# Value projection of cached samples moved into a feed-forward block, key products on one engine, finals two steps apart

## The chip, the cores and the metric

The kernel runs on one core of a Trainium2 chip. The time is device microseconds of one execution. The core has five engines that each work through their own list of instructions in order: TensorE (PE, matmuls), VectorE (DVE), ScalarE (ACT), GpSimd (POOL) and SyncE (SP), which here issues all the DMAs. The engines meet at semaphores.

## The reference

One layer of a hybrid decoder for 2048 prompt tokens and 32 sample rows (8 samples with 4 new tokens each), D = 1024, everything in float32:

```python
z = rmsnorm(x, g) @ w_in                     # -> q, k, v (8 heads x 64), u, vg (512 each)
# attention in three branches (window, dilation) = (128,1), (512,4), (2048,16),
# merged by their softmax denominators; samples see a cache of 2048 keys and values:
s = einsum('bthc,btjhc->bthj', q, k_all[:, idx]) * 64**-0.5 + bias
o = einsum('bthj,btjhc->bthc', exp(s - lse), v_all[:, idx])
gate = einsum('gts,...sgc->...tgc', tril(w_s), layernorm(vg)) + b_s
x = x + concat(att, u * gate) @ w_out
x = x + (silu(h @ w_gate) * (h @ w_up)) @ w_down     # h = rmsnorm(x, g), 2816 hidden columns
y = rmsnorm(x, final_g)
```

The outputs are y for prompt and samples, the prompt's keys and values, the samples' caches moved on by four rows, and the samples' normalised vg.

## The kernel before

Each float32 product is made of three matmuls: both operands are split into a high part (a copy rounded for PE, on ACT) and a low part (original minus high, on DVE or POOL). The order on every engine is written out by hand: the scheduler only adds the semaphores. The stages are these.

- **Input projection**, 240 steps of one 128-row slice of `w_in` against three or so token tiles, a little over two microseconds each. The rest of the stage's work is put at steps by `at(step, phase, function)`: a `Plan` sorts by step, then by phase ("early", "turn", "mid", "out", "misc", "store" among ten), and calls the functions in that order. The functions only append to the engines' lists. Here also lie the spatial gate (layer norm, split into `vnh`, `vnl`, gate matmuls L426, eviction `gates_u` L434) and the samples' attention.
- **Samples' attention.** 96 key units (8 samples x 4 tokens x 3 branches): a product of cached keys with the broadcast query on DVE or POOL (L555), and a sum over each head's 64 columns on DVE (L560). Two softmaxes follow for four samples each. Then 72 value units (9 for a sample: one near piece, and far and middle pieces for 4 tokens): load of 96 to 128 rows x 512, high part on ACT (L629), low part on DVE or POOL (L635), two matmuls (L644, L645) that add into one PSUM bank for the nine. The stationary operand is the split probabilities (`z0`, `z1`); a mask and a small selecting matmul make the sample's four output rows of it.
- **Prompt attention**, then three token **blocks** of 6, 6 and 4 tiles. Each has output projection, second norm and the feed-forward's gate and up products. These go by 22 slices `f` of the hidden columns, and a slice has seven products `q` = 0..6 (a Strassen form): a *slot* is one product, 12 matmuls of 384 columns in the first block (L1686 to L1688). Each slot's product is evicted or added by DVE or ACT (L1698 q = 1, L1700 q = 2, L1710 q = 3, L1713 and L1714 q = 4, L1716 q = 5, L1723 and L1748 q = 6), and between them lie the operand sums (L1603 to L1612, DVE), high parts (L1619, ACT) and low parts (L1623, POOL) for the next slice.
- **Down projection** of all blocks (class `Down`): stages of ten steps with 12 matmuls each. Step `n` also splits the operands of step `n + 3` (L1883 to L1886); after each stage the first four steps evict its four banks, and in the last stages of each half they also start a final norm each (`final`, L1811, L1457, L1818).

Small PSUM tiles come from `ps_t()`, which takes the banks in `ring` in turn. `roll(1)` copies a piece of up to 512 KB of the samples' cache from input to output, DRAM to DRAM.

Of the kernel before, what the change touches and what calls it, by code (L numbers as in the profile page):

```python
# [66 lines left out]
def hymba_step(ctx: ExitStack, tc: tile.TileContext, A: dict, O: dict):  # L67
# [55 lines left out]
    t_d = dram.tile([NJ, 2, P, 2, 512], F32, name="t_d")  # L123
    x1_d = dram.tile([T, D], F32, name="x1_d")
# [359 lines left out]
    bias_s = gp.tile([P, 3, 1, ST * H], F32, name="bias_s")  # L484
# [40 lines left out]
    sel = sp.tile([2 * SR, ST], F32, name="sel")  # L525
# [36 lines left out]
    def sample_start():  # L562
        dve.memset(S, 0.0)
        sync.dma_start(sel, A["sel"])

    def values_start():


        unit["z0"] = z0 = sp.tile([P, 2, ST, 2, ST, H], F32R, name="z0", tag="kn", bufs=2)
        dve.memset(z0.bitcast(F32), 0.0)  # L570

    def head_mask():
        unit["hm"] = sp.tile([P, DA], F32, name="hm", tag="kn", bufs=2)[0:2 * SR]
        sync.dma_start(unit["hm"], A["headmask"])
# [24 lines left out]
    def softmax_c(bg):  # L599
# [4 lines left out]
        unit["pT", bg] = pT = sp.tile([P, 3, 4, ST, H], F32, name="pT", tag="pT", bufs=1)  # L604
        act.activation(pT.rearrange("p u b t h -> p (u b t h)"), pt[:, 0:3 * P], AF.Copy)

    def probabilities(b):
        pT = unit["pT", b // 4]
        bi = b % 4
        z0 = unit["z0"]  # L610
        for u in range(2):

            hi = bass.AP(tensor=z0.tensor, offset=z0.offset + u * ST * 2 * SR, ap=[list(z0.ap[0]), [2 * SR + H, ST], [1, H]])
            lo = bass.AP(tensor=z0.tensor, offset=z0.offset + u * ST * 2 * SR + SR, ap=[list(z0.ap[0]), [2 * SR + H, ST], [1, H]])
            dve.tensor_copy(hi, pT[:, u, bi])
            dve.tensor_sub(lo, pT[:, u, bi], hi.bitcast(F32))

    def near_probabilities(b):
        pT = unit["pT", b // 4]
        bi = b % 4  # L620
        unit["z1"] = z1 = sp.tile([P, 2, ST * H], F32R, name="z1", tag="z1", bufs=1)
        src = pT[:, 2, bi].rearrange("p t h -> p (t h)")
        dve.tensor_copy(z1[:, 0, :], src)
        dve.tensor_sub(z1[:, 1, :], src, z1[:, 0, :].bitcast(F32))

    def value_unit_split(b, i, u, t):
# [11 lines left out]
    def value_unit(b, i, u, t):  # L638
        vh, vl, n = unit.pop(("vs", b, i))
        if i == 0:  # L640
            unit["po"] = ps_t(1)
# [1184 lines left out]
    class Down:  # L1826
# [98 lines left out]
        def run(self):  # L1925
            for n in range(2 * NS - TAIL):
# [495 lines left out]
```

## Time and profile before

| | before |
|---|---|
| runs: median (lowest to highest) | 2494.89 us (2493.87 to 2495.75) |
| profiled execution, its time | 2493.14 us |
| profiled execution, span from first to last instruction | 2491.4 us |
| mean granted PE clock | 0.992 |

The span by stages, with PE's busy time, from the table by stretches:

| stretch, us | stage | length | PE busy | DVE | ACT | POOL |
|---|---|---|---|---|---|---|
| 0–575 | input projection | 575 | 548.4 | 338.8 | 257.3 | 216.3 |
| 575–935 | prompt attention | 360 | 321.8 | 289.4 | 260.0 | 207.1 |
| 1000–1310 | block 1 of 3, gate and up | 310 | 309.9 | 188.2 | 116.4 | 198.9 |
| 1410–1735 | block 2 of 3, gate and up | 325 | 324.3 | 231.1 | 125.5 | 222.7 |
| 1815–2070 | block 3 of 3, gate and up | 255 | 255.0 | 169.1 | 136.0 | 198.0 |
| 2070–2491 | down projection, finals | 421.4 | 401.3 | 320.1 | 190.3 | 7.6 |

In the rows below, `L635 DVE TENSOR_TENSOR vl<-kv,vh` is an instruction of line 635 on DVE that writes `vl` from `kv` and `vh`. A row of a list of waits ends with three numbers: the time that the engine waited for this in all, how often, and the longest. A row of the timeline begins with its start in us and its length, and ends, in brackets, with the time its engine had been idle and what ended that. A row of a group ends with its count, busy us and mean ns of one, and the idle time ahead of it with what released it.

### The profile page before, as it was taken

Reading aid. Unit: us, or ns where it says so; the run is one execution under the profiler, and the core shown is the slowest. Engines: PE = TensorE matmul, PEld = TensorE weight load, DVE = VectorE, ACT = ScalarE, POOL = GpSimd, SP = SyncE. Lnnn points to the kernel's source line nnn. Section 1 sums busy time; section 2 is a strip of 40 time slices with the busy share of each in tenths; the row PEclk is TensorE's granted clock in tenths of the full one; section 3 lists DMA queues with packets and bytes.
Section 4 is the critical chain, followed back from the end, with each engine's and each line's share of the span. In section 5 each row is a group of like instructions: output and inputs, shape, how many; then the busy total and the mean of one; then the engine's idle time right before and its main releaser. Section 6 shows DMA issues by size and latency. Waiting matters only on the chain. (4 is left out here: it accounts for less than half of the span.)

```text
span 2491.4 us, 39127 instructions
## 1 busy us (share of the span) xinstructions
PE 2397.9 (96%) x13358; PEld 2120.8 (85%) x13358; DVE 1691.0 (68%) x3081; ACT 1211.9 (49%) x2385; POOL 1183.7 (48%) x909
## 2 busy tenths in 40 slices
PE   8999999999989889999999999999999999999997
PEld 6787777778888777999998899999799998887886
DVE  4368686446878777656655776776566666877876
ACT  6414344546877656433333633334455554445444
POOL 1145643224575746666663576666467881000000
PEclk9999999999999999999999999999999999999999
DMA  8863854788788665566659177666647776755832
GB/s 265 255 202 112 275 147 140 246 278 265 232 281 259 218 185 171 190 212 207 202 200 320 36 250 255 231 243 226 255 151 229 234 221 235 279 186 197 318 128 89
DMA packets 315221, 537.17 MB, mean 216 GB/s; under 512 B 28417, under 2 KB 151714, under 8 KB 309134
## 3 DMA queue, kind: packets, MB, share of 16 engines
q1 hardware_dynamic: 310060, 526.16, 64.6%
q10 hardware_dynamic: 4962, 8.51, 1.3%
q8 instruction: 106, 1.74, 0.3%
q14 instruction: 93, 0.76, 0.1%
HBM read 418.41 MB, written 186.28 MB: 243 GB/s over the span
## 5 line engine op out<-in xcount | busy, mean ns | idle before, releaser
L1686 PE MATMUL ps_m<-xh,op 128*128 128x384 f32 (+5 forms) x1932 | 612.3, 317 | 0.8 <-DVE raw L1714 0.5
L1687 PE MATMUL ps_m<-xl,op 128*128 128x384 f32 (+5 forms) x1932 | 612.0, 317 | 0.0
L1688 PE MATMUL ps_m<-xh,op 128*128 128x384 f32 (+5 forms) x1932 | 611.3, 316 | 0.0
L1623 POOL TENSOR_TENSOR op<-fr,op 128x512 fp32r<-128x512 f32 x286 | 402.6, 1424 | 91.7 <-ACT op L1619 65.0
L1686 PEld LDWEIGHTS ps_m<-xh,op 128*128 128x128 f32 x1932 | 363.9, 188 | 2.4 <-issue 0.8
L1687 PEld LDWEIGHTS ps_m<-xl,op 128*128 128x128 f32 x1932 | 363.8, 188 | 0.6
L1688 PEld LDWEIGHTS ps_m<-xh,op 128*128 128x128 f32 x1932 | 364.2, 188 | 0.0
L1623 POOL TENSOR_TENSOR op<-pair,op 128x512 fp32r<-128x512 f32 x126 | 169.6, 1347 | 158.3 <-DVE hr L1748 87.1
L1619 ACT ACTIVATE op<-fr 128x512 fp32r<-128x512 f32 x330 | 196.6, 621 | 12.2 <-PE ps_m L1438 6.0
L335 PE MATMUL ps_s<-wh,xh 128*128 128x512 f32 x480 | 195.8, 408 | 6.1 <-ACT xh L139 6.1
L336 PE MATMUL ps_s<-wl,xh 128*128 128x512 f32 x480 | 189.9, 396 | 0.0
L337 PE MATMUL ps_s<-wh,xl 128*128 128x512 f32 x480 | 189.5, 395 | 0.1
L1737 ACT ACTIVATE ps_t<-zn 128x384 f32<-128x384 f32 (+2 forms) x132 | 60.0, 454 | 250.4 <-DVE zn L1716 205.5
L1883 ACT ACTIVATE op<-fr 128x512 fp32r<-128x512 f32 x140 | 88.3, 631 | 173.9 <-issue 89.2
L1955 POOL TENSOR_TENSOR ac<-ac,final_g 128x512 f32<-128x512 f32 x2 | 2.6, 1296 | 351.9 <-DMA fr<-t_d 349.3
L1885 DVE TENSOR_TENSOR op<-fr,op 128x512 fp32r<-128x512 f32 x140 | 99.3, 710 | 80.4 <-ACT op L1883 80.1
L1619 ACT ACTIVATE op<-pair 128x512 fp32r<-128x512 f32 x126 | 79.0, 627 | 110.9 <-DVE pair L1609 110.9
L335 PEld LDWEIGHTS ps_s<-wh,xh 128*128 128x128 f32 x480 | 91.5, 191 | 34.5 <-issue 7.3
L1900 PE MATMUL ps_m<-op 128*128 128x512 f32 x280 | 109.0, 389 | 0.9 <-ACT op L1884 0.9
L1902 PE MATMUL ps_m<-op 128*128 128x512 f32 x280 | 109.1, 390 | 0.2
L337 PEld LDWEIGHTS ps_s<-wh,xl 128*128 128x128 f32 x480 | 91.5, 191 | 20.8 <-POOL xl L142 0.5
L1901 PE MATMUL ps_m<-op 128*128 128x512 f32 x280 | 109.0, 389 | 0.0
(551 smaller groups left out, 5942.0 us busy)
## 6 DMA issues: line engine op xcount, KB each, us to landing
fr<-in_w_gate_dram SPq DMA_DIRECT2D x132, 256.0 KB
out_ks_dram<-in_cache_k_dram SPq DMA_DIRECT2D x56, 512.0 KB
out_vs_dram<-in_cache_v_dram SPq DMA_DIRECT2D x56, 512.0 KB
fr<-in_w_up_dram SPq DMA_DIRECT2D x110, 256.0 KB
fr<-ab_d SPq DMA_DIRECT2D x88, 256.0 KB
a<-h_d SPq DMA_DIRECT2D x80, 256.0 KB
fr<-t_d SPq DMA_DIRECT2D x80, 256.0 KB
raw<-in_w_in_dram SPq DMA_DIRECT2D x72, 256.0 KB
```

What stands on the lines that cost most here:

```text
L335: pe.matmul(o[j], xh[:, k, :], wh, start=(k == 0), stop=False)
L336: pe.matmul(o[j], xh[:, k, :], wl, start=False, stop=False)
L337: pe.matmul(o[j], xl[:, k, :], wh, start=False, stop=(k == KD - 1))
L1619: act.activation(ops[f, j][0], ab[f][j], AF.Copy)
L1623: (eng or pool).tensor_sub(lo_, ab[f][j], hi.bitcast(F32))
L1686: pe.matmul(out, wh[:, ks], xh[:, :, k], start=(k == 0), stop=False)
L1687: pe.matmul(out, wh[:, ks], xl[:, :, k], start=False, stop=False)
L1688: pe.matmul(out, wl[:, ks], xh[:, :, k], start=False, stop=(k == 3))
L1885: dve.tensor_sub(wl, w, wh.bitcast(F32))
L1900: pe.matmul(banks[m], hh[:, ts], wh, start=first, stop=False, skip_group_check=more)
L1901: pe.matmul(banks[m], hh[:, ts], wl, start=False, stop=False, skip_group_check=more)
L1902: pe.matmul(banks[m], hl[:, ts], wh, start=False, stop=j == NJ - 1, skip_group_check=more)
```

## The change

- **Value units.** Loads, splits and matmuls of the 72 units leave steps 160 to 241 of the input projection. They now stand in the first block's slices 1 to 21: with `x = 7 f - 7 + q`, unit `k` has its two matmuls in slot `9 + 16k // 9`, straight after that slot's product. Its high part (ACT) is two slots earlier, its low part one slot earlier and always on DVE, its load in the slot before that of unit `k - 2`, whose staging buffer it takes. The probabilities go through a DRAM tile `p_d`. The mask is 64 x 8 and is broadcast over each head's columns.
- **Key units.** All 96 products are on DVE (57 were on POOL). From the thirteenth on they stand at steps 63, 64.9, 66.8 … 222, where before they came in bursts of 0.4 to 1.7 a step up to step 162. The softmaxes stand at steps 150 and 227 (158 and 189 before).
- **Banks.** The ring for `ps_t` is [0, 1] up to step 168 and [0, 1, 3] up to 240. Before it was [0] from 165 and [0, 3] from 168, since the values held bank 1.
- **Rolls.** 21 cache copies go from the first block to steps 172 to 222 of the input projection.
- **Samples' gate.** The load and the eight small transposes of the samples' gate values go from the prompt attention to the second block's slice 19.
- **Finals.** `Down` evicts the four banks of a stage at steps 0, 2, 4 and 6 of the next (0 to 3 before), and the finals go with them. The four little tiles of squares share one.

PE's order around the gates of step 166 to 168, before and after (the number behind `ps_t` is the bank; `vnh` is the layer norm's high part, `wg_h` the gate's weights, `vh`, `vl` a value unit). Before:

```order
L426 MATMUL ps_t0_3515<-vnh_3276,wg_l_107 128x256
L335 MATMUL ps_s_3365<-wh_3079,xh_2810 128x512
...
L337 MATMUL ps_s_3365<-wh_3079,xl_2863 128x512
L426 MATMUL ps_t0_3553<-vnh_3276,wg_h_106 128x256
...
L337 MATMUL ps_s_3365<-wh_3096,xl_2863 128x512
L644 MATMUL ps_t1_3570<-vh_3476,z1_3449 64x512
L645 MATMUL ps_t1_3570<-vl_3497,z1_3449 64x512
L335 MATMUL ps_s_3585<-wh_3398,xh_2305 128x512
```

After:

```order
L427 MATMUL ps_t0_3331<-vnh_3118,wg_l_108 128x256
L336 MATMUL ps_s_3201<-wh_2915,xh_2684 128x512
...
L338 MATMUL ps_s_3201<-wh_2915,xl_2737 128x512
L427 MATMUL ps_t1_3359<-vnh_3118,wg_h_107 128x256
...
L338 MATMUL ps_s_3201<-wh_2937,xl_2737 128x512
L336 MATMUL ps_s_3386<-wh_3233,xh_2220 128x512
```

The second gate's bank changes from 0 to 1, and the value unit's two matmuls behind it are gone.

DVE's order a few steps later, past the gates (`om` is a sample's masked output, `z` its probabilities, `un` the gated u). Before:

```order
L635 TENSOR_TENSOR vl<-kv,vh 128x512
L649 TENSOR_TENSOR om<-ps_t_3570,hm 64x512
L615 CAST z_3209<-pT 128x4x8
L616 TENSOR_TENSOR z_3209<-pT,z_3209 128x4x8
...
L635 TENSOR_TENSOR vl<-kv,vh 100x512
L434 SCALAR_TENSOR_TENSOR un<-ps_o_3833,sgb,un 128x4x64 x2
```

After:

```order
L555 TENSOR_TENSOR pr<-kv,qb 96x512
L560 TENSOR_REDUCE S_s<-pr 96x8
L555 TENSOR_TENSOR pr<-kn,qb 128x512
L435 SCALAR_TENSOR_TENSOR un<-ps_o_3586,sgb,un 128x4x64 x2
L560 TENSOR_REDUCE S_s<-pr 128x8
L555 TENSOR_TENSOR pr<-kv,qb 100x512
```

Values' low parts and probabilities make room for key products (L555) and their sums (L560).

DVE's order in the first block at the turn from one slice to the next (`zn`, `raw` and `hr` are the products' evictions and the hidden values, `pair` and `fr` the operand sums of the next slice). Before:

```order
L1716 TENSOR_TENSOR zn<-zn,ps_m_10982 128x384
L1748 TENSOR_TENSOR hr<-ps_t_10996,raw 128x3x2x64
L1723 TENSOR_TENSOR raw<-raw,ps_m_11002 128x384
L1748 TENSOR_TENSOR hr<-ps_t_10934,raw 128x3x2x64
L1603 TENSOR_TENSOR pair<-fr 128x512
L1606 TENSOR_TENSOR fr<-fr 128x512
L1698 TENSOR_TENSOR raw<-zn,ps_m_11048 128x384
```

After (L2213 is a value unit's low part, lines 1645 and 1670 were 1723 and 1748, line 1525 was 1603, line 1620 was 1698):

```order
L1638 TENSOR_TENSOR zn<-zn,ps_m_10440 128x384
L1670 TENSOR_TENSOR hr<-ps_t_10454,raw 128x3x2x64
L1645 TENSOR_TENSOR raw<-raw,ps_m_10463 128x384
L1670 TENSOR_TENSOR hr<-ps_t_10378,raw 128x3x2x64
L2213 TENSOR_TENSOR svb<-sva,svb 100x512
L1525 TENSOR_TENSOR pair<-fr 128x512
L1528 TENSOR_TENSOR fr<-fr 128x512
L1620 TENSOR_TENSOR raw<-zn,ps_m_10514 128x384
```

A low part stands between the slice's last eviction and the first operand sum; its matmuls on PE (L2221, L2222) come after the next product.

The diff, cut to its core:

```diff
-    for s0, r in ((165, [0]), (168, [0, 3]), (B0, [0, 1])):
+    for s0, r in ((168, [0, 1, 3]), (B0, [0, 1])):
...
-    key_steps = [46 + 5 * i // 4 for i in range(8)] + [60, 61, 61, 62] + [63 + int(i / 1.7) for i in range(17)]
-    key_steps += [73 + int(i / 1.2) for i in range(12)] + [83 + int(i / 0.4) for i in range(11)] + [111 + int(i / 0.95) for i in range(32)]
-    key_steps += [145 + int(i / 0.7) for i in range(12)]
+    key_steps = [46 + 5 * i // 4 for i in range(8)] + [60, 61, 61, 62] + [63 + 19 * i // 10 for i in range(84)]
...
-        at(s0, "out", key_unit, b, t, u, pool if u == 1 or u == 2 and not 83 <= s0 < 111 and s0 < 150 else dve)
+        at(s0, "out", key_unit, b, t, u, dve)
...
-    V0 = 166
     for bg in range(2):
-        s0 = (V0 - 8, V0 + 23)[bg]
+        s0 = (150, 227)[bg]
+        at(s0 - 1, "early", sample_bias, bg)
         at(s0, "turn", softmax_a, bg)
         at(s0 + 1, "early", softmax_e, bg)
         at(s0 + 2, "mid", softmax_b, bg)
-        at(s0 + (5 if bg else 4), "turn", softmax_c, bg)
-    for b in range(SB):
-        s0 = V0 + 9 * b
-        at(s0 - 3, "misc", near_probabilities, b)
-        at(s0 + 1, "early", probabilities, b)
-        for i, (u, t) in enumerate([(2, 0)] + [(u, t) for u in range(2) for t in range(ST)]):
-            at(s0 + i - 6, "misc", unit_load, ("v", b, i), A["cache_v"], 2, u, b, t)
-            at(s0 + i - 2, "out", value_unit_split, b, i, u, t)
-            at(s0 + i - 1, "mid", value_unit_low, b, i, u, t)
-            at(s0 + i + 1, "out", value_unit, b, i, u, t)
-        at(s0 + 10, "early", sample_out_a)
-        at(s0 + 11, "turn", sample_out_b)
-        at(s0 + 12, "early", sample_out_c, b)
+        at(s0 + 4, "turn", softmax_c, bg)
+        at(s0 + 6, "store", softmax_d, bg)
+    for y in range(21):
+        at(172 + 5 * y // 2, "store", roll, 1)
...
@@ the down projection @@
-                if n >= NJ and j < 4:
+                m = j // 2
+                if n >= NJ and j % 2 == 0 and m < 4:
                     phv, ps_, _ = self.at(n - j - 1)
-                    self.evict(phv, ps_, j, self.prev)
+                    self.evict(phv, ps_, m, self.prev)
                     if ps_ == 5:
-                        self.final(phv * 8 + 2 * j)
+                        self.final(phv * 8 + 2 * m)
                     if ps_ == 6:
-                        self.final(phv * 8 + 2 * j + 1)
+                        self.final(phv * 8 + 2 * m + 1)
                     if hv == 1 and s == 5:
-                        self.square_half(j)
+                        self.square_half(m)
...
@@ the value units in the first block @@
+    def probabilities(b, u):
+        z0, src = vals["z0"], of_probabilities(u, b)
+        hi, lo_ = (bass.AP(tensor=z0.tensor, offset=z0.offset + y * SR, ap=[list(z0.ap[0]), [2 * SR + H, ST], [1, H]]) for y in range(2))
+        dve.tensor_copy(hi, src)
+        dve.tensor_sub(lo_, src, hi.bitcast(F32))
...
+    def value_load(k, b, u, t):
+        x, n, base = vals["x"][:, k % 2], ROWS[u], b * WB * DA
+        if u == 0:
+            sync.dma_start(x[0:NFAR], dap(A["cache_v"], base + t * DA, [[16 * DA, NFAR], [1, DA]]))
...
+    def value_high(k, u):
+        n = ROWS[u]
+        act.activation(vals["vh"][0:n, k % 2], vals["x"][0:n, k % 2], AF.Copy)
+    def value_low(k, u):
+        n = ROWS[u]
+        dve.tensor_sub(vals["vl"][0:n, k % 2], vals["x"][0:n, k % 2], vals["vh"][0:n, k % 2].bitcast(F32))
+    def value_unit(k, i, u, t):
+        n = ROWS[u]
+        if i == 0:
+            vals["po"] = ps_o()
+        po = vals["po"]
+        lt = vals["z1"] if u == 2 else vals["z0"][:, t * 2 * SR:(t + 1) * 2 * SR]
+        pe.matmul(po[0:2 * SR], lt[0:n], vals["vh"][0:n, k % 2], start=(i == 0), stop=False)
+        pe.matmul(po[0:2 * SR], lt[0:n], vals["vl"][0:n, k % 2], start=False, stop=(i == 8))
...
+        VORDER = [(2, 0)] + [(u, t) for u in range(2) for t in range(ST)]
+        when = lambda k: 9 + 16 * k // 9
+        vat(0, values_start)
+        vat(2, values_probabilities, 0)
+        for k in range(SB * 9):
+            b, i = k // 9, k % 9
+            u, t = VORDER[i]
+            x = when(k)
+            vat(when(k - 2) - 1, value_load, k, b, u, t)
+            vat(x - 2, value_high, k, u)
+            vat(x - 1, value_low, k, u)
+            if i == 0:
+                vat(x - 1, near_probabilities, b)
+            elif i in (1, 5):
+                vat(when(k - 1), probabilities, b, u)
+            vat(x, value_unit, k, i, u, t)
+            if k == 4 * 9 - 3:
+                vat(x, values_probabilities, 1)
+            if i == 8:
+                vat(x + 1, sample_out_a)
+                vat(x + 3, sample_out_b)
+                vat(x + 4, sample_out_c)
+                vat(x + 5, sample_out_d, b)
...
+            if bi == 0 and f:
+                for fn, args in vplan.get(f * 7 - 7 + q, ()):
+                    fn(*args)
+            if bi == 1 and f == 19 and q == 1:
+                sgu_sample_cat_load()
+            if bi == 1 and f == 19 and q == 4:
+                sgu_sample_cat()
...
-            if f + 1 < NF and q in (1, 4)[:(1, 2, 0)[bi]]:
+            if f + 1 < NF and q in (1, 4)[:(0, 2, 0)[bi]]:
```

More of the change, by code (lines that the diff above doesn't have):

```diff
@@ L563, in sample_start @@
         dve.memset(S, 0.0)
[L564 to L574, printed above, removed]
     def sample_bias(bg):
@@ L1150, in sgu_sample_cat @@
         c = sgu.pop("c")
-        pt = ps_t()
+        pt = ps_o()
         for a in range(2):
```

107 lines of the change are left out of this document (51 added, 56 removed).

## The prediction, written before the changed kernel was run

> **What bounds the kernel now.** I read the page first: TensorE (PE) is busy nearly all the time, so an edit counts only where PE waits, or where it makes PE wait anew.
>
> ```profile
> span 2491.4 us, 39127 instructions
> PE 2397.9 (96%) x13358; PEld 2120.8 (85%) x13358; DVE 1691.0 (68%) x3081; ACT 1211.9 (49%) x2385; POOL 1183.7 (48%) x909
> ```
>
> Next the stretches that the change touches. The columns are us from the start, length, then busy us of PE, its weight loads, DVE, ACT and POOL with their instruction counts, the granted clock, the DMA share and GB/s.
>
> ```profile
> 200.00:250.00 50.00, 46.13 (x231) 37.65 (x230) 42.22 (x91) 25.57 (x45) 29.41 (x21) 0.97 0.41 123
> ...
> 300.00:350.00 50.00, 49.51 (x212) 40.88 (x213) 40.17 (x53) 14.17 (x21) 24.36 (x16) 0.97 0.78 226
> 350.00:400.00 50.00, 41.50 (x185) 32.81 (x184) 44.39 (x101) 28.07 (x51) 24.42 (x19) 0.90 0.26 81
> ...
> 1030.00:1290.00 260.00, 260.00 (x1502) 260.00 (x1501) 156.13 (x233) 95.52 (x179) 163.98 (x126) 1.00 0.64 209
> ...
> 2446.00:2491.00 45.00, 30.47 (x123) 23.45 (x121) 29.53 (x74) 19.11 (x42) 0.00 (x0) 0.89 0.27 100
> ```
>
> The input projection (first 575 us) has holes at 200–250 and 350–400, and DVE is 84% and 89% busy there. The first feed-forward block, where the value work goes, has none: PE 260 of 260. It also has the fuller POOL: 164 of 260, 63%. The waits of PE name what it waited for (us in all, count, the longest):
>
> ```profile
> PE ps_t L426 <- DVE un L434: 5.8, 2, 5.0
> PE ps_t L426 <- ACT vnh L139: 4.5, 2, 2.9
> PE ps_o L335 <- DVE zn L459: 3.7, 1, 3.7
> PE ps_t L353 <- ACT zn L347: 3.0, 2, 1.7
> PE ps_t L426 <- POOL vnl L142: 2.0, 2, 1.0
> ```
>
> L426 is the matmul of the spatial gate, L434 its eviction, L459 the normalised sample rows, L347 the eviction that feeds the gate's layer norm.
>
> **Input projection, the gate's bank.** The order of the gates shows two of them on bank 0 one after the other, because the values' accumulator held bank 1:
>
> ```profile
> 376.68 1.75 DVE L635 TENSOR_TENSOR vl<-kv,vh 128x512 fp32r<-128x512 f32 x1
> 379.17 0.74 DVE L393 SCALAR_TENSOR_TENSOR zn<-zn,mv,lng 128x512 f32<-128x512 f32 x1
> 380.49 0.87 DVE L434 SCALAR_TENSOR_TENSOR un<-ps_t,sgb,un 128x256 f32<-128x256 f32 x2
> 381.41 0.58 PE L426 MATMUL ps_t<-vnh,wg_h 128*128 128x256 f32 x1 [5.00 <-DVE un L434]
> ```
>
> The second gate cannot start before L434 has emptied the bank, and L434 stands in DVE's queue behind a value's low half and a layer norm. Afterwards the second gate has bank 1, and the low half is gone from DVE: 5.0 us come back. The granted clock of this stretch is 0.90, so 10% of 50 us, 5 us of full clock, are lost; part of that falls into the hole itself. I count half, 2.5. Gain **7.5**, between 5.0 and 10.0. The Trainium skill (TensorE: Matmul & The Clock Gate, What's actually happening) says that an idle window of some 3.4 us puts the clock to half for at least as long; by it the hole drags 1.7 or 3.4 us along, and the sum would be 6.7 or 8.4. The trace's 0.90 agrees with a loss of that kind.
>
> **The layer norm's chain.** The waits on vnh, vnl and zn add up to 4.5 + 2.0 + 3.0 = 9.5 us, at 213 us and at 364–374 us, and the clock of 0.97 in 200–250 adds 1.5: 11.0. Two things lengthen that chain, the table load for the softmax's exponential just ahead of an L347, and key products and their sums on DVE:
>
> ```profile
> 361.61 1.28 ACT L592 ACT_TABLE_LOAD   x1
> 364.00 0.68 ACT L347 ACTIVATE zn<-ps_s,rstd 128x512 f32<-128x512 f32 x1
> ...
> L560 DVE TENSOR_REDUCE S_s<-pr 96x8 f32<-96x512 f32 x28 | 18.8, 673 | 1.8 <-POOL pr L555 1.8
> L555 DVE TENSOR_TENSOR pr<-kv,qb 100x512 f32<-100x512 f32 x27 | 32.5, 1203 | 11.9 <-DMA qb<-zs_d 9.3 <-DMA kv<-in_cache_k_dram 1.6 <-DVE S_s L560 1.0
> L555 POOL TENSOR_TENSOR pr<-kv,qb 96x512 f32<-96x512 f32 x32 | 47.8, 1494 | 61.4 <-DMA qb<-zs_d 28.3 <-DMA kv<-in_cache_k_dram 21.7 <-DVE S_s L560 6.7
> L555 POOL TENSOR_TENSOR pr<-kn,qb 128x512 f32<-128x512 f32 x25 | 40.2, 1609 | 5.9 <-DMA kn<-in_cache_k_dram 4.6 <-DVE S_s L560 1.2
> L635 DVE TENSOR_TENSOR vl<-kv,vh 100x512 fp32r<-100x512 f32 x16 | 12.0, 756 | 0.0
> ```
>
> The softmax moves from step 158 to 150, away from the last gate group. In steps 63–93, ahead of the gates at 213 us, 33 units are due before; 13 of their products are on DVE (13 x 1.20) and all their sums (33 x 0.67), 38 us. After the change 16 units are due there, wholly on DVE, at 0.76 for a product (the L635 row, two operands of 512 columns from SBUF like it) and 0.67 for a sum: 23 us. DVE loses 15 us of work in some 70 us, ahead of the very chain that is late. Over the whole stage it is no gift: the 57 products that POOL had cost DVE 57 x 0.76 = 43 us (68 at 1.20), and the 40 low halves that leave save about 40 x 0.8 = 32. That I take 0.76 rests on POOL: its 47.8 + 40.2 us of products and 32 low halves leave, and the same kind of operation took 1.20 beside them. I count 60% of the 11.0: **6.6**, between 0 and 11.
>
> **The sample rows at 300 us.**
>
> ```profile
> 295.14 3.46 DVE L142 TENSOR_TENSOR xl<-xr,xh 128x1024 fp32r<-128x1024 f32 x1 [1.25 <-ACT xh L139]
> 298.52 1.27 DVE L560 TENSOR_REDUCE S_s<-pr 128x8 f32<-128x512 f32 x2
> 299.71 0.73 DVE L459 SCALAR_TENSOR_TENSOR zn<-ps_o,rstds,zn 32x512 f32<-32x512 f32 x1
> 300.49 0.80 PE L335 MATMUL ps_o<-wh,xh 128*128 128x512 f32 x1 [3.73 <-DVE zn L459]
> ```
>
> PE waits 3.7, and 0.97 of clock in 300–350 costs 1.5 more: 5.2. L459 stands behind a split of 3.46 and two sums. Here 0.95 unit a step become 0.53, and no product runs on POOL beside the split. I count three quarters, **3.9**, between 1.5 and 5.2. Together the input projection gives -18.0, between -6.5 (5.0 + 0 + 1.5) and -26.
>
> **First feed-forward block: the stall that the values bring.** The 144 matmuls are the same in number and size, so PE's work only moves. What counts is whether a low half is ready when its slot's product ends, since PE has no reserve here. Before, in the input projection, the low half came two steps ahead and the list of waits has no PE wait for it. Now it is one slot ahead, and a slot is about 2.07 us (1102.63 to 1104.71 below).
>
> ```profile
> 1102.63 0.56 DVE L1700 TENSOR_TENSOR zn<-zn,ps_m 128x384 f32<-128x384 f32 x1 [0.85 <-PE ps_m L1688]
> 1104.71 0.56 DVE L1710 TENSOR_TENSOR zn<-raw,ps_m 128x384 f32<-128x384 f32 x1 [1.52 <-PE ps_m L1688]
> ...
> 1110.95 0.56 DVE L1723 TENSOR_TENSOR raw<-raw,ps_m 128x384 f32<-128x384 f32 x1 [0.35 <-PE ps_m L1688]
> 1111.54 0.56 DVE L1748 TENSOR_TENSOR hr<-ps_t,raw 128x384 f32<-128x384 f32 x1
> 1111.90 1.29 POOL L1623 TENSOR_TENSOR op<-fr,op 128x512 fp32r<-128x512 f32 x1
> 1112.02 1.72 DVE L1603 TENSOR_TENSOR pair<-fr 128x512 f32<-128x512 f32 x1
> ...
> L1603 DVE TENSOR_TENSOR pair<-fr 128x512 f32<-128x512 f32 x18 | 31.0, 1720 | 0.0
> L1609 DVE TENSOR_TENSOR pair<-fr 128x512 f32<-128x512 f32 x17 | 11.6, 684 | 0.0
> L1623 POOL TENSOR_TENSOR op<-fr,op 128x512 fp32r<-128x512 f32 x72 | 95.8, 1343 | 26.2 <-ACT op L1619 26.2
> ```
>
> In most slots the low half starts behind one eviction, 0.56 after the product's end, and lasts 0.68 (L1609): done at 1.24 of 2.07. In a slot's last position (q = 6; likewise q = 4, which has two evictions) it starts 1.1 after, behind L1723 and L1748. At q = 6 that is the very place where L1603 takes 1.72 every time, 18 times over, against 0.68 for its twin L1609: POOL's L1623 began at 1111.90 and ends at 1113.19, and L1603 ends 0.55 after that. The low half now stands at that place, ends at 1113.74, which is 2.79 after 1110.95, and the next product is done 2.07 after it: 0.72 late. Unit k has slot 9 + 16k//9, so 11 of the 72 low halves fall on q = 6 and 11 on q = 4: 11 x 0.72 = 8, 11 x 0.2 = 2.2 where POOL may or may not be in the way, and 0.8 for eight batches' near probabilities: **+11**, between 0 and +29 (0.4 for each of the 72). The 18 late L1603 hurt nobody before, since what they make is used slots later; the low half has a consumer at once. ACT gains 72 copies at about 0.6 (43 us on 95.5 of 260), DVE 72 low halves and the splits (some 56 on 156), neither over 82%.
>
> **Finals.** Each final costs DVE an eviction, a newton step and a product with its waits, between the operand splits:
>
> ```profile
> 2450.33 0.16 DVE L1457 TENSOR_SCALAR s<-s 128x1 f32<-128x1 f32 x1 [1.22 <-ACT pair L1811]
> 2451.28 0.69 DVE L1885 TENSOR_TENSOR op<-fr,op 128x512 fp32r<-128x512 f32 x1 [0.79 <-ACT op L1883]
> ...
> 2454.03 1.28 DVE L1818 SCALAR_TENSOR_TENSOR ac<-ac,s,final_g 128x1024 f32<-128x1024 f32 x1
> 2455.23 0.15 DVE L1457 TENSOR_SCALAR s<-s 128x1 f32<-128x1 f32 x1
> ```
>
> From one L1457 to the next are 4.9 us for one step, two splits (1.2) among them; a step's twelve matmuls take 2.7. Four in a row put DVE 4 x 2.2 = 8.8 late. At every second step it needs 4.9 + 1.2 + a further wait of about 1.2 = 7.3 against 5.4, four times 1.9 = 7.6 late. That is hardly less, so **0**, between -4 and +4. Moved rolls, sample transposes and bias: 0, between -1 and +2; the rolls take over the cache loads' share of DMA, 0.26 to 0.78 in these stretches.
>
> **The sum.** -18 + 11 + 0 = -7. The profiled execution took 2493.14 (span 2491.4), so 2486; the median of the runs is 1.75 above it: **2488**.
>
> **Rivals.** (1) Slower: POOL's products block the low halves wherever they stand. With POOL 63% busy and 1.34 a product, a low half that starts at random waits 0.63 x 0.67 = 0.42; if nothing absorbs it, 72 x 0.4 = 29, and -18 + 29 gives 2506. It decides from 18 / 72 = 0.25 us a unit on. Against it: outside q = 4 and 6 there are 0.83 us to spare. The Trainium skill (SBUF — State Buffer, Who interferes with whom) has the rule that speaks against this change: a DVE instruction with two inputs in SBUF waits for the whole GpSimd instruction that began first; L1603's 1.72 agrees. (2) No change: the layer norm's chain keeps its waits because DVE is as full as before, now with the keys; -7.5 - 1.5 + 11 gives 2496. For it: the net of DVE's work above is +11 us. (3) More: the block's slack hides every low half and the spaced finals return a few us: -18 - 3 gives 2474.
>
> **How the numbers follow.** Forecast 0.42, rival 1 0.18, rival 2 0.22, rival 3 0.18. The range 2475 to 2504 leaves out most of rival 1's upper half and the lower part of rival 3; the forecast's own is 2481 to 2495. What a measurement here can tell from no change is 0.2%, 5 us: faster is under 2489.9, slower over 2499.9. Faster: rival 3 and most of the forecast, 0.53; same: the rest of the forecast and most of rival 2, 0.24; slower: rival 1 and a rest of rival 2, 0.23.
>
> **What would show it.** Right: no wait of the gate on L435 (L434 before), clock 1.00 in 350–400, shorter waits on vnh and zn; in the block, PE waits for svb at L2222, some 0.7 each, at q = 6 only. Wrong: waits at L2222 in most units (rival 1), the waits on vnh as before (rival 2), none at L2222 (rival 3), or PE waits in places that I did not name, such as on the keys' queries, on SP behind the value loads, or at the softmax beside the last steps.

## The result: 1.2% slower

The changed kernel takes 2524.09 us (median, 2521.39 to 2532.07), the kernel before 2495.32 beside it: a ratio of 1.0118, 95% interval 1.0092 to 1.0144. The forecast was 2488 with a range to 2504. The profiled execution took 2523.58 us, its page begins so:

```profile
span 2521.8 us, 38932 instructions
...
PE 2409.6 (96%) x13358; PEld 2127.7 (84%) x13358; DVE 1727.2 (68%) x3169; ACT 1210.2 (48%) x2385; POOL 1070.1 (42%) x821
```

POOL has 114 us less to do and DVE 36 us more. PE is busy 12 us more with the same number of matmuls of the same sizes.

**Where the time went.** The table holds lengths of stages in the two profiled executions, by the starts of their first and last matmuls in the timeline. "Value work" is the time from the starts of the 160 moved matmuls to the starts of those behind them, 43 us in either place; the pauses between them are in it.

| stage | before | after | difference | less value work |
|---|---|---|---|---|
| input projection | 577.0 | 546.0 | -31.0 | **+12** |
| prompt attention to the first product | 410.8 | 409.4 | -1.4 | -1.4 |
| first block, products | 326.6 | 388.3 | +61.7 | **+18.7** |
| second block, products | 327.2 | 328.4 | +1.2 | +1.2 |
| third block, products | 261.3 | 261.3 | 0 | 0 |
| down projection and finals | 420.0 | 420.1 | +0.1 | +0.1 |

The table by stretches of the changed kernel (us from the start, length, busy us of PE, weight loads, DVE, ACT, POOL, clock, DMA share, GB/s):

```profile
200.00:250.00 50.00, 49.30 (x254) 39.87 (x253) 43.65 (x94) 24.09 (x43) 22.49 (x16) 1.00 0.45 136
...
300.00:350.00 50.00, 50.00 (x225) 41.33 (x224) 32.36 (x66) 17.85 (x29) 4.81 (x4) 1.00 0.45 138
350.00:400.00 50.00, 45.34 (x216) 37.06 (x215) 44.18 (x86) 20.84 (x37) 18.16 (x13) 0.97 0.41 130
400.00:450.00 50.00, 42.15 (x200) 34.60 (x200) 23.94 (x41) 15.46 (x25) 0.00 (x0) 0.90 0.82 268
450.00:500.00 50.00, 41.28 (x180) 33.39 (x179) 17.90 (x29) 11.16 (x18) 0.00 (x0) 0.93 0.88 278
500.00:546.00 46.00, 43.62 (x199) 35.80 (x198) 10.69 (x19) 13.62 (x22) 8.92 (x7) 1.00 0.86 307
```

The kernel before, from 400 us on:

```profile
400.00:450.00 50.00, 49.62 (x251) 37.95 (x250) 23.70 (x40) 24.96 (x43) 15.07 (x12) 1.00 0.54 165
450.00:500.00 50.00, 48.52 (x217) 35.68 (x216) 20.01 (x42) 23.08 (x39) 10.38 (x8) 1.00 0.84 262
500.00:550.00 50.00, 50.00 (x223) 37.16 (x222) 24.44 (x39) 26.35 (x46) 14.47 (x11) 1.00 0.84 264
```

Up to 400 us the change does what was expected of it: PE is busy 49.3, 50.0 and 45.3 of 50 us where it was 46.1, 49.5 and 41.5, and the clock is 1.00, 1.00 and 0.97 instead of 0.97, 0.97 and 0.90. Now count as loss what the time from one matmul's start to the next is longer than usual for its shape (the median in the kernel before, 0.227 us for 128x512). In 200 to 400 us this loss falls from 24.8 to 10.0. From 400 us to the projection's end it rises from 6.0 to 26.2 us; ahead of 200 us it is 3.4 higher. These add up to some 9 us and not to the table's 12, mainly because the 43 us taken off there hold 2.6 us of loss in the kernel before. PE's list of waits names both new losses (us in all, count, longest):

```profile
PE ps_t L354 <- ACT zn L348: 15.8, 5, 6.8
...
PE ps_o L2221 <- DVE z L2193: 6.2, 4, 2.9
PE ps_o L2221 <- DVE z L2187: 6.1, 8, 1.2
...
PE ps_o L354 <- ACT zn L348: 5.1, 2, 4.0
...
PE ps_o L427 <- ACT vnh L140: 1.9, 1, 1.9
...
PE ps_o L2222 <- DVE svb L2213: 0.3, 1, 0.3
PE ps_t L427 <- DVE un L435: 0.2, 1, 0.2
```

The gate's wait on its bank (L434 before, L435 now) is down from 5.8 to 0.2 us. New are 20.9 us for zn, the copy of a projection result on ACT that PE transposes (L348, L354), and 12.3 us in the first block for z, the split probabilities. For the low halves svb PE waits 0.3.

**The wait for zn is a wait for DMA.** The timeline of ACT and PE around the longest one:

```profile
431.01 0.72 ACT L233 ACTIVATE wh<-raw,g1c 128x512 fp32r<-128x512 f32 x1 [5.08 <-DMA raw<-in_w_in_dram]
433.09 0.60 ACT L359 ACTIVATE pair<-ps_t 128x512 fp32r<-128x512 f32 x1 [1.36 <-DMA qk_d<-pair]
434.75 0.72 ACT L233 ACTIVATE wh<-raw,g1c 128x512 fp32r<-128x512 f32 x1 [1.07 <-DMA raw<-in_w_in_dram]
437.03 0.72 ACT L233 ACTIVATE wh<-raw,g1c 128x512 fp32r<-128x512 f32 x1 [1.56 <-DMA raw<-in_w_in_dram]
...
437.66 0.67 ACT L348 ACTIVATE zn<-ps_s,rstdn 128x512 f32<-128x512 f32 x1
...
438.38 1.11 PE L354 MATMUL ps_t<-ident,zn 128*128 128x128 f32 x4 [6.78 <-ACT zn L348]
```

L348 has its input in PSUM since 431.6 at the latest, when the last matmul ahead of it ended. But it stands in ACT's queue behind three high halves of weights (L233) and a pair (L359). Each high half starts as its weights land, at 430.9, 434.7 and 437.0. ACT's own waits in 400 to 520 us:

```profile
ACT wh L233 <- DMA raw<-in_w_in_dram: 26.0, 12, 5.1
ACT pair L359 <- DMA qk_d<-pair: 24.8, 5, 13.0
```

Before, the first of these was a quarter, and the second was 1.6 us (400 to 577 us):

```profile
ACT wh L232 <- DMA raw<-in_w_in_dram: 6.1, 4, 2.1
```

The second row is the other way for a late DMA to hold ACT: L359 writes the pair of tiles whose last content a store to `qk_d` must first have taken away. From the end of its issue to its last landing, a weight load took 4.9 us (median of 16) in 390 to 520 us, 3.8 in the kernel before.

**The wait for z is a wait for POOL's port.** DVE in the first block, and the product on POOL beside it:

```profile
1036.82 0.67 DVE L2213 TENSOR_TENSOR svb<-sva,svb 128x512 fp32r<-128x512 f32 x1
1037.42 1.24 DVE L2192 CAST z<-sva 128x32 fp32r<-128x32 f32 x1
1038.69 1.20 DVE L2193 TENSOR_TENSOR z<-sva,z 128x32 fp32r<-128x32 f32 x1
...
1035.43 3.19 POOL L1545 TENSOR_TENSOR op<-fr,op 128x512 fp32r<-128x512 f32 x2 [0.36 <-ACT op L1541]
...
1040.04 0.42 PE L2221 MATMUL ps_o<-svb,z 128*64 128x512 f32 x1 [2.25 <-DVE z L2193]
```

A cast of 32 columns takes 1.24 us, and its subtraction 1.20; the same two took 0.17 and 0.19 at 996.55 us, with POOL idle. The cast ends with POOL's pair of products at 1038.6, the subtraction with the next at 1039.84. The low half of 512 columns right ahead of them took 0.67 us and did not wait. Of POOL's products, the one beside that low half took 1.93 us, those before and behind it 1.31 and 1.25, so there it seems to have been POOL that waited.

### The profile page after: what moved, and what is told of

It reads as the page before. It is cut to its first block, busy times and chain, and to the rows that moved or that the text cites. A ratio compares the mean times of both kernels' runs of the same rounds, so it can differ in the third digit from the quotient of the medians.

```text
span 2521.8 us, 38932 instructions
## 1 busy us (share of the span) xinstructions
PE 2409.6 (96%) x13358; PEld 2127.7 (84%) x13358; DVE 1727.2 (68%) x3169; ACT 1210.2 (48%) x2385; POOL 1070.1 (42%) x821
## 5 line engine op out<-in xcount | busy, mean ns | idle before, releaser
L1545 POOL TENSOR_TENSOR op<-fr,op 128x512 fp32r<-128x512 f32 x286 | 413.3, 1461 | 101.9 <-ACT op L1541 69.9
```

The costliest lines, as they stand in the source:

```text
L1545: (eng or pool).tensor_sub(lo_, ab[f][j], hi.bitcast(F32))
```

## The experiments

Each ratio is to runs of the kernel before on the same chip. Lengths of stages are read from the profiled executions as above, and losses are counted as above. One profile is one execution: kernels with the same code in a stage gave 544.4 to 546.0 us for the input projection (three kernels), 387.0 to 394.0 for the first block's products (seven), and 409.1 to 420.7 for the prompt attention. Differences inside these bounds show nothing by themselves.

### The copies back in the first block

```diff
-    for y in range(21):
-        at(172 + 5 * y // 2, "store", roll, 1)
...
-            if f + 1 < NF and q in (1, 4)[:(0, 2, 0)[bi]]:
+            if f + 1 < NF and q in (1, 4)[:(1, 2, 0)[bi]]:
```

> The changed kernel with its 21 cache copies back in the first feed-forward block, one a slice, as before the change. Theory (the copies crowd the weight loads of the input projection: these land 5 to 6.5 us after issue, and ScalarE starts on each the moment it lands): the waits of PE for zn (L348), 21 us in the changed kernel, fall below 5, the input projection ends about 22 us sooner (546 to about 524), the time falls from 2523.6 to about 2502, a little more if the copies disturb the block's value loads. Rival (the key loads with their query broadcasts, or SP's stores that wait for the gate, make the weights late): the waits for zn stay above 15 us and the time within 6 us of 2523.

Measured: 2516.99 us, ratio 1.0099 (1.0078 to 1.0120). The projection ends at 527.8 instead of 546.0, 18 us sooner, a weight load lands after 3.65 us instead of 4.9 (medians of 16), and the waits for zn fall from 20.9 to 8.3. End, waits and time all fall by less than the theory had:

```profile
PE ps_t L354 <- ACT zn L348: 8.1, 3, 4.5
...
PE ps_o L354 <- ACT zn L348: 0.2, 1, 0.2
```

The median falls by 7 only: in the profiled execution the attention is 6 us longer than in the changed kernel (415.7), and the first block 4.5 (392.8). Both lie inside what these stages vary by, so it is not shown that the copies in the first block gave the rest back. It is shown that they cost the projection 18 us.

### The copies on GpSimd's queue

```diff
-            sync.dma_start(O[dst][b, r0:r1, :], A[src][b, ST + r0:ST + r1, :])
+            queue.dma_start(O[dst][b, r0:r1, :], A[src][b, ST + r0:ST + r1, :])
...
-        at(172 + 5 * y // 2, "store", roll, 1)
+        at(172 + 5 * y // 2, "store", roll, 1, pool)
```

> The changed kernel with the 21 copies at the same steps of the input projection, but issued from GpSimd's queue instead of SyncE's. If the copies hurt by their place in SyncE's queue (the weights' issues stand behind them), the waits for zn fall below 8 us and the time to about 2505; if they hurt by their traffic (weights land late whoever issues), the weights still land 5 us or more after issue, the waits for zn stay above 14 us and the time within 8 us of 2523.

Measured: 2535.16 us, ratio 1.0178 (1.0155 to 1.0201), and no answer. POOL has nothing else to do there and issued the copies one after another, 21 in 31 us, without the pace of the steps:

```profile
397.87 0.49 POOL L170 DMA_DIRECT2D out_ks_dram<-in_cache_k_dram  x1 [1.51 <-DMA out_ks_dram<-in_cache_k_dram]
399.58 0.49 POOL L170 DMA_DIRECT2D out_ks_dram<-in_cache_k_dram  x1 [1.22 <-DMA out_ks_dram<-in_cache_k_dram]
```

In the burst a key load landed 26 us after the end of its issue, and PE had one hole of 18.0 us. It shows what the copies' traffic can do, not what their queue does.

### The splits of the probabilities earlier

```diff
-    def probabilities(b, u):
+    def probabilities(b, u, t0):
...
+        src = src[:, t0:t0 + 2]
...
-                vat(x - 1, near_probabilities, b)
+                vat(x - (2 if b == 4 else 4), near_probabilities, b)
...
-                vat(when(k - 1), probabilities, b, u)
+                lead = 3 if i == 1 else 2
+                vat(max(when(k - lead), {1: 6, 37: 71}.get(k, 0)), probabilities, b, u, 0)
+                vat(max(when(k - lead + 2), {1: 6, 37: 71}.get(k, 0)), probabilities, b, u, 2)
```

> The changed kernel with the splits of the probabilities (z0 in two halves, z1) moved two to four slots ahead of the value unit that reads them; the low halves stay where they are. Theory (in the first block PE waits for these tiny splits, which take 1.2 us instead of 0.2 while a GpSimd product runs): PE's waits for z fall from 12.3 us to below 2, the block's loss from 18.7 to about 5, the time to about 2510. Rival (the low halves of the values are late too and take over, or the loads): new waits at L2221 and L2222 of more than 8 us and a time within 6 us of 2523.

Measured: 2509.96 us, ratio 1.0076 (1.0057 to 1.0096), 14 us below the changed kernel. The first block's products take 374.5 us instead of 388.3, well outside what this stage varies by. PE has no wait for z left, and the low halves do not take over:

```profile
PE ps_o L2223 <- DVE svb L2214: 2.6, 4, 1.2
```

The splits themselves became no faster (the casts, twice as many, 0.79 us on average); they have time now. The theory holds.

### The finals as before

```diff
-                m = j // 2
-                if n >= NJ and j % 2 == 0 and m < 4:
+                m = j
+                if n >= NJ and m < 4:
```

> The changed kernel with the evictions and finals of the down projection at the first four steps of a stage again. Theory (spacing them trades one long lag for four short ones; the down stage takes 420.1 us in both kernels): the stage from the last product to the end stays within 2 us of 420.1 and the time within 3 us of 2523.6. Rival (the spacing does pay and something else in that stage takes it away, or it costs): a difference of 5 us or more.

Measured: 2526.04 us, ratio 1.0131 (1.0111 to 1.0150), 2 us from the changed kernel and inside its runs. From the last product to the end it is 421.0 us against 420.1. Spacing the finals neither gives nor costs what could be seen here.

### Key products on GpSimd again

```diff
-        at(s0, "out", key_unit, b, t, u, dve)
+        at(s0, "out", key_unit, b, t, u, pool if u == 1 or u == 2 and s0 >= 76 else dve)
```

> The changed kernel with 57 of the 96 key products on GpSimd again (all 32 of the middle branch, 25 of the near one), at the new steps. Theory (the gain at 200 to 310 us comes from thinner key work, and from DVE no longer sharing its port): DVE's own two-operand operations lengthen again from 0.7 towards 1.2 us, PE's waits for the layer norm at 213 us and for the sample rows at 300 us come back in part, 3 to 8 us, and the time rises to 2526 to 2532. Rival (only the spacing counts): PE's lost time between 200 and 340 us stays below 4 us and the time within 3 us of 2523.

Measured: 2526.91 us, ratio 1.0140 (1.0117 to 1.0163). The time alone does not decide: it lies in the theory's range, yet its difference of 2.8 us to the changed kernel is inside the runs of both. The projection ends at 542.6, 3.4 us sooner. The rows of its stretches:

```profile
200.00:250.00 50.00, 47.39 (x248) 38.47 (x247) 41.71 (x92) 23.92 (x42) 31.12 (x22) 1.00 0.47 139
...
350.00:400.00 50.00, 46.89 (x240) 39.17 (x239) 37.23 (x81) 21.31 (x38) 27.16 (x20) 1.00 0.44 136
```

PE is busy 2 us less at 200 to 250 and 1.5 us more at 350 to 400. The loss is 3.9 us in 200 to 340 (2.3 in the changed kernel), just under the rival's bound, and 8.0 in 200 to 400 against 10.0, where the kernel before had 24.8. DVE's key products of 100 rows lengthen from 0.89 to 1.08 us, as the theory had it. So the engine is worth some 2 us either way and is not what gave the gain. The keys' spacing, the bank, the softmax's new step and the values' splits that left are not told apart by this run.

### One more step of lead for the weights

```diff
-        W[n, "r"] = r = raw_tile()
+        W[n, "r"] = r = raw_tile() if n % 4 < 3 else sp.tile([P, 512], F32, name="wr", tag="wr", bufs=1)
...
-        pr = sp.tile([P, DA], F32, name="pr", tag="pr", bufs=5)
+        pr = sp.tile([P, DA], F32, name="pr", tag="pr", bufs=4)
...
-        at(need - 9, "misc", w_load, n)
+        at(need - 10, "misc", w_load, n)
```

> The changed kernel with a fourth staging buffer for the input projection's weights (in place of one of the five for the key products) and each weight load one step earlier, four steps ahead of its high part instead of three. Theory (the lead is counted in steps, and a step from 166 on lost its value unit, 0.46 of 2.5 us, so three steps are 6.1 us now for loads that land 5 to 6.5 us after issue): with four steps the waits of PE for zn fall from 21 us below 10 and the time to 2508 to 2514, the copies staying where they are. Rival (it is the copies' traffic alone, more loads in flight land later): the waits stay above 16 us and the time within 5 us of 2523.6.

Measured: 2521.26 us, ratio 1.0115 (1.0100 to 1.0131). The projection ends 7 us sooner (538.8), the waits for zn fall to 16.4. As written, the rival holds, for the waits stay above 16 us and the time within 5. But the 7 us by which the projection ends sooner are more than it varies by. ACT now waits longer for the other DMA:

```profile
ACT pair L359 <- DMA qk_d<-pair: 38.0, 8, 12.1
...
ACT wh L233 <- DMA raw<-in_w_in_dram: 11.2, 4, 4.8
```

Weights that wait less leave ACT waiting for the stores (38.0 instead of 24.8 us). The lead of the weights is a part of the loss, not the whole.

### The kernel before without most of the values' matmuls

```diff
+        if i not in (0, 8):
+            return
         pe.matmul(po[0:2 * SR], lt[0:n], vh[0:n], start=(i == 0), stop=False)
```

> The kernel before, with the two matmuls of seven of every nine value units left out (112 matmuls, 25.8 us of PE, at steps 166 to 241; the samples' attention is then not the reference's). Loads, splits and copies stay where they are. Theory (the value matmuls gave the weight loads time): without them PE waits anew for zn or for the low halves, 5 us or more, and the time falls by less than 20 us, to 2474 or more. Rival (their PE time covered nothing): it falls by 24 to 28 us, to 2466 to 2470.

Measured: 2476.78 us, ratio 0.9936 (0.9920 to 0.9953), 16 us less. As written, the theory holds: a wait for zn of 5.1 us appears (7.4 in all, 3.0 before), and the time falls by less than 20. But most of what the time falls short by lies elsewhere, since the attention behind took 418.7 us instead of 410.8. The projection itself ends 25.0 us sooner for 25.8 us of PE work taken out. From 400 us on its loss rises from 6.0 to 11.8 us, and ahead of that it falls by 5.3, in part where nothing was edited. So without the copies the value units' PE work covers some 6 us there.

### The copies in the kernel before

```diff
+    for y in range(21):
+        at(172 + 5 * y // 2, "store", roll, 1)
...
-            if f + 1 < NF and q in (1, 4)[:(1, 2, 0)[bi]]:
+            if f + 1 < NF and q in (1, 4)[:(0, 2, 0)[bi]]:
```

> The kernel before with one part of the change alone: its 21 copies go from the first feed-forward block to steps 172 to 222 of the input projection; values and keys stay. Theory (copies beside the weight loads are the price): PE waits anew for zn (L347), 8 us or more in 400 to 580, and the projection, 577 us in the kernel before, ends at 590 or later; the first block stays at 326.6; time 2504 to 2520. Rival (the copies hurt only together with the other parts, since steps with a value unit are longer): the projection ends before 583 and the time stays under 2499.

Measured: 2498.95 us, ratio 1.0027 (1.0013 to 1.0041). The projection ends at 581.2, 4 us later, though a weight load lands later here too (4.6 us after its issue, 3.8 without the copies). So the rival holds, and the same 21 copies that cost 18 us in the changed kernel cost 4 here, at the same steps and with the DMA engines as full:

```profile
450.00:500.00 50.00, 47.15 (x205) 34.88 (x204) 18.69 (x39) 22.25 (x38) 9.78 (x8) 0.97 0.95 311
500.00:550.00 50.00, 49.20 (x218) 36.08 (x217) 24.84 (x41) 25.38 (x43) 12.93 (x10) 1.00 1.00 322
```

DMA is busy 0.95 and 1.00 of the time, more than the 0.82 to 0.88 of the changed kernel, and PE waits for zn 5.4 us in all.

### The copies on ScalarE's queue

```diff
-        at(172 + 5 * y // 2, "store", roll, 1)
+        at(172 + 5 * y // 2, "store", roll, 1, act)
```

> The changed kernel with the 21 copies at the same steps, issued from ScalarE's queue instead of SyncE's, so that they keep their pace. If their place in SyncE's queue makes weights and stores late, PE's waits for zn (L348) fall from 21 us below 10 and the time to 2505 to 2512. If it is their traffic, the waits stay above 15 us and the time within 6 us of 2523.6, or rises, since ScalarE also spends the time of their issue.

Measured: 2530.30 us, ratio 1.0148 (1.0121 to 1.0175). The projection ends at 545.0, and PE's waits for zn stay:

```profile
PE ps_t L354 <- ACT zn L348: 18.1, 6, 8.0
...
PE ps_o L354 <- ACT zn L348: 5.4, 3, 3.8
```

From ScalarE's queue the copies cost the projection what they cost from SyncE's, so their place in SyncE's queue is not the cause. (SyncE does not issue all the other DMAs: in both kernels ScalarE issues the 32 broadcasts of the samples' queries, `qb`.)

### PE work back in the steps

```diff
+        if 169 <= ((half * 5 + ki) * 3 + gi) * 8 + k:
+            if "pad" not in outs:
+                outs["pad"] = bank(1)
+            for z in range(2):
+                pe.matmul(outs["pad"][0:64], xT[half * 8][0][:, k, 0:64], wh, start=True, stop=True)
...
-    for s0, r in ((168, [0, 1, 3]), (B0, [0, 1])):
+    for s0, r in ((169, [0, 3]), (B0, [0, 1])):
```

> The changed kernel with two matmuls of 64 x 512 without use added to every step from 169 on (142 matmuls, some 33 us of PE, as much as the value units had there; their bank is 1, so that the ring is 0 and 3 from step 169 as before). If the length of a step is what covers the copies, the waits for zn fall from 21 us below 8, the projection ends at 560 to 568 instead of 546 + 33 = 579, and the time is 2537 to 2545. If the traffic costs the same whatever the steps' length, the waits stay above 15 and the time is 2553 to 2560.

Measured: 2540.40 us, ratio 1.0186 (1.0153 to 1.0218). With 33 us of work added, the projection ends at 557.9, 12 us later: 21 of the 33 us lay in what had been waiting.

```profile
PE ps_t L359 <- ACT zn L353: 6.1, 3, 2.6
...
PE ps_o L359 <- ACT zn L353: 2.7, 1, 2.7
```

The waits for zn (20.9) are 8.8 now, a little over the bound; end and time lie inside or below what the theory gave. The granted clock in 400 to 500 us is 1.00 instead of 0.90 and 0.93, so part of the 21 us is clock that the holes had cost. The losses from 400 us to the projection's end, side by side:

| loss, us | without copies | with copies |
|---|---|---|
| kernel before | 6.0 | 10.0 |
| kernel before without most of the values' matmuls | 11.8 | not run |
| changed kernel | 12.1 | 26.2 |
| changed kernel with PE work added to its steps | not run | 12.8 |

This settles the cause: it is the copies' traffic together with the shorter steps. A step with a value unit lasts 0.46 us longer, and all that a step must load and store has that much more time to land.

### Three losses mended at once

The copies go to the third block (`(0, 2, 1)` in place of `(0, 2, 0)`, none in the projection), with the early splits and the longer lead from above.

> The changed kernel with three edits: the 21 copies go to the third feed-forward block, the splits of the probabilities two to four slots earlier, the weights' fourth buffer and one more step of lead. Theory (the three losses are apart): input projection 20 to 24 us shorter than in the changed kernel, first block 13 to 14 shorter, third block unchanged, time 2486 to 2492, level with the kernel before or up to 0.3% faster. Rival (they share one cause, DMA traffic that only moves on): the third block or the prompt attention grows by 5 us or more and the time stays over 2497.

Measured: 2490.49 us (ten runs, 2484.67 to 2496.82), ratio 0.9994 (0.9983 to 1.0004): level with the kernel before, 34 us below the changed one. The projection ends at 520.9, 25 us sooner, the first block takes 375.6 (-12.7), the third 261.5 with its 21 copies (261.3 without). The attention takes 413.7. PE's list has 3.8 us for zn, and for the low halves

```profile
PE ps_o L2221 <- DVE svb L2212: 3.8, 7, 1.2
```

The losses are apart, as expected: what is taken out of one stage does not come back in another.

### Two more edits on top

```diff
-        at(s0, "out", key_unit, b, t, u, dve)
+        at(s0, "out", key_unit, b, t, u, pool if 154 <= s0 < 178 else dve)
```

> The version with three edits (copies in the third block, early splits, a fourth weight buffer), and the key products of steps 154 to 177 on GpSimd instead of DVE. Theory (the 4 to 7 us that are still lost at 360 to 390 us come from keys on DVE ahead of the gates' layer norm): the loss in 350 to 400 falls from 7.5 to 4 or less, the time from 2490.5 to 2486 to 2488. Rival (the chain is late for another reason): loss and time unchanged within 2 us.

Measured: 2488.01 us, ratio 0.9980 (0.9968 to 0.9991). The loss in 350 to 400 falls from 7.5 to 4.5, the projection ends 3 us sooner (517.9). DVE is busy 38.5 us there instead of 40.8. PE is as busy as before (46.6 and 46.5 us), but the clock is 1.00 instead of 0.93. The time is 2.5 us less, and the intervals of the two ratios overlap, so a gain in time is not shown:

```profile
350.00:400.00 50.00, 46.59 (x237) 38.86 (x236) 38.48 (x80) 21.12 (x38) 28.41 (x22) 1.00 0.40 117
```

Then the attention's copies:

```diff
-    for y in range(25):
-        at(B0 + 20 + 5 * y, "store", roll, 1)
+    for y in range(12):
+        at(B0 + 20 + 10 * y, "store", roll, 1)
...
-            if f + 1 < NF and q in (1, 4)[:(0, 2, 1)[bi]]:
+            if f + 1 < NF and q in (1, 4)[:(0, 2, 2)[bi]]:
```

> The version with three edits, and 13 of the prompt attention's 25 copies taken out of it (the third block takes two a slice instead of one). Theory (the attention stage, 409 to 411 us in both kernels and 413.7 in this version, is slowed by its DMA traffic): it falls to 408 or less, the third block stays within 1 us of 261.4, the time falls to 2483 to 2487. Rival (the attention waits for its own engines, not for DMA): it stays within 2 us of 413.7 and the time within 2 us of 2490.5.

Measured: 2488.66 us, ratio 0.9976 (0.9964 to 0.9988). The attention takes 410.9, 2.8 us less, the third block 263.3, 1.8 more; the time is 1.8 us less, inside the rival's bound. Not settled.

> Both of the last two edits together. If each gives what its theory says and they are apart, the time is 2479 to 2484, 0.4 to 0.5% below the kernel before. If neither does, 2488 to 2492.

Measured: 2482.78 us (2480.36 to 2489.71), ratio 0.9965 (0.9951 to 0.9978). This version is 0.35% faster than the kernel before and by these ratios 1.5% faster than the change; it is 7.7 us below the version with three edits, more than the 4.3 that the two gave one by one, which the scatter of the runs allows. Its attention takes 409.1, its third block 261.4.

```profile
span 2479.2 us, 38971 instructions
```

## Why the prediction was wrong

**The gate's bank, the layer norm, the sample rows (-18).** The mechanism was right and the size nearly: the loss between 200 and 400 us fell by 14.8. The 5.0 us wait on L434 is gone, the hole at 300 us is closed, and the hole at 213 us too. What stayed is 7.6 us in 350 to 400 (12.1 before), the gates of the last group. The reason I gave for one price was beside the point: keys on DVE without POOL beside them. With the keys back on POOL the gain stays. Near the last gates the loss is even smaller with keys on POOL, 4.1 to 4.5 us in 350 to 400. How much the spacing gave, and how much the softmax's new step and the values' splits that left, was not told apart.

**Moved copies (0, between -1 and +2).** This is the step that failed. I set the copies against the cache loads that leave, and quoted DMA shares of 0.26 to 0.78, but these were shares of 200 to 400 us. The copies went to 400 to 546 us, where the share of the kernel before was already 0.54 to 0.84. Nor did I ask which transfers of the projection have little time: the weights, three steps ahead of their high halves, with three buffers. From 400 us to the projection's end the loss rose by 20 us, and taking the copies away ended the projection 18 us sooner.

**"PE's work only moves."** I counted the 43 us of value work as neutral and looked only at where it arrives. Where it leaves it had made the steps longer: 2.5 us with a value unit, 2.04 without. In the loss from 400 us on, the copies alone cost 4.0 us (kernel before) and the shorter steps alone 5.8, both together 20.2. None of my rivals had this, and the range ended 20 us too low.

**The first block (+11, up to 29).** Place and mechanism were right: a POOL product that holds DVE up ahead of a value unit. The sum was 18.7 (17.4 to 24.4 over the kernels that leave the block so) and not 11, because I put the stall on the wrong instruction. The low halves were on time (0.3 us), also at q = 6, where I expected 0.72 each; 12.3 us went to the splits of the probabilities, which I had priced at 0.8 for the near ones and at nothing for the others. With these splits earlier 4.9 of the 18.7 us stay, 2.6 of them waits for low halves. One of their own rows shows why:

```profile
L2186 DVE CAST z<-sva 128x32 fp32r<-128x32 f32 x16 | 11.5, 718 | 0.0
```

The cast takes 0.17 us when POOL is idle and 0.72 on average. In this trace a short instruction pays the same remainder of POOL's product as a long one, and two of them in a row can pay twice. The Trainium skill (SBUF — State Buffer, Who interferes with whom) lists casts, under conditions on their operands, among the instructions that can take the port shared with GpSimd, beside those with two SBUF inputs; the trace agrees, 1.24 us for the cast that began beside POOL's product. I had used the page for operands of two inputs only.

**Finals (0).** Right: 420.0 us before, 420.1 after, 421.0 with the old spacing.

**The rivals.** The slower one named the block and bounded its price at 29 us, but it needed waits for the low halves in most units. A slower kernel was given 0.23. That was too low for six edits, several of which put new work next to engines or queues whose leads are counted in steps. Waits in places that I did not name were on my list of signs against the forecast, and the waits for zn behind the weights and for z were such.

**Still open.** The attention stage has the same matmuls in all these kernels and took between 409.1 and 420.7 us. Among the changed kernel's variants it was longer in several whose projection ended sooner (413 to 417 us), but longest of all behind the one that ended 12 us later. With 13 copies less it was 2.8 us shorter in one pair of profiles and 7.8 in another. How much of it is DMA left over from the projection was not told apart.

## What to carry to other kernels

Work that leaves a stage takes its time with it: whatever is due a fixed number of steps ahead (loads, stores that free a buffer) has less time after, so price a stage that gets shorter by its transfers' landing times, before anything is added to it. When traffic moves, ask which transfers of its new place have the least lead, not what share of the DMA engines is free. And give tiny preparations the same lead as large ones, since beside a busy GpSimd they cost almost as much.

## What the runs showed of the hardware

- A DVE cast of 128x32 takes 0.17 us alone and 1.24 beside a GpSimd product; the subtraction behind it 0.19 and 1.20.
- With DMA engines busy 0.95 and 1.00 of the time PE waited little (loss of 5.5 and 2.2 us in 50), and with 0.82 to 0.88 it lost 11 and 12 us in 50: the share does not tell whether transfers are on time.
- Copies from DRAM to DRAM issued without a pace, 21 in 31 us, made one load land 26 us after its issue.
- With 21 such copies spread over some 125 us, a weight load of 256 KB landed 4.9 us after its issue, without them 3.65 (medians of 16).
